# A hybrid decoder block on one Trainium2 core: transposes tied to emitted weight pieces, moves on GpSimd's queue, a gate and a z block in one product, and a shorter last root

## The chip, the cores and the metric

The kernel runs on one core of one Trainium2 chip, in one launch. The metric is the device time of one execution in microseconds (us); the time before is 1645.88 us, the median of three runs (1645.79 to 1647.56). Engines are called as in the profile: PE (TensorE, matrix products), DVE (VectorE), ACT (ScalarE), POOL (GpSimd) and SP (SyncE, which here only starts transfers). An engine, and a queue of transfers that it starts, takes its instructions in order.

## The reference

One layer over 256 tokens (two halves of 128, called t = 0 and 1), width D = 2048, all in float32. The three branches are sliding-window attention with sinks, a multi-scale pooling mixer and a Mamba-2 SSD mixer; the parts around the change are these:

```python
h = rmsnorm(x, ln1_w)
q, k, v, u, z, xbc, dt_raw, gate_logits = split(h @ w_in)
ssm = ssd_mixer(z, xbc, ...)
# in ssd_mixer: g = (y * silu(z)) in 4 groups of 512 columns,
#               g * rsqrt(mean(g*g) + EPS) * norm_w
gates = sigmoid(gate_logits)            # 3 x 2048
merged = gates[0] * (att @ w_attn_br) + gates[1] * (pool @ w_pool_br) \
       + gates[2] * (ssm @ w_ssm_br)
x = x + merged @ w_out
gu = rmsnorm(x, ln2_w) @ w_gate_up
x = x + (silu(gu[:, :F]) * gu[:, F:]) @ w_down
return rmsnorm(x, final_w)
```

## The kernel before

**Products.** Every float32 product is made of three passes in a rounded float32 form: each operand is cut into a high and a low part, and PE does high x high, high x low and low x high (`three`, L225 to L227). Weights arrive in pieces of two 128-row slices by 512 columns. For each piece ACT casts the high part `whi` and DVE subtracts it to get `wlo` (`split`, L139 to L147). `weights` (L149) has three buffers for the arriving `raw` and five each for `whi` and `wlo`. One piece is 2 slices x 2 token halves x 3 passes = 12 matmuls of 512 columns. A block is 512 output columns over K = 2048, that is 8 pieces or 96 matmuls.

**Double blocks.** `two_blocks` (L315) makes two blocks of 512 columns at once. For two of the eight pairs of slices it uses seven products in place of eight, so 21 matmuls where plain pieces have 24. Its banks are: q1 and q7 from the pool `tr`, q5 and q6 from `sm`, q2, q4, q3 and q8 from the four banks of `acc`. The operand's combinations (`block_forms`) are made once per operand as side work. The weights' combinations come through `sraw`, which has one buffer, and `vu` (`block_weights`, L288 on): `whi` and `wlo` of the first half of `sraw`, a DVE sum `vu`, its split, two more sums and two more splits.

**Transposes of activations.** A result has tokens on the partitions, and the next product needs its columns there. `turn` (L487 to L514) does this for a block of 512 columns: sixteen transfers of 32 KB put 32x128 pieces into `mid` (`move`), then DVE does two stream transposes into `tt` (L502) and four splits with a scale follow (`parts`; on ACT these are the rows `ssm_hi<-tt`). Turned are the SSD result `ys` (tile `y`, through `ssm`), the merged sum `m4`, the residual `x2` (tile `x`) and the FFN's product `ff`.

**Side work.** `later` appends work to a list, `pause` appends an empty entry with a cost, and `side(share)` is called once for each weight piece: it takes the first entry if there is credit. A turn is `move`, then `pause(5)` (moves on SP) or `pause(12)` (moves on POOL), then `parts`; whatever stands behind a pause in the list waits too. `finish_tasks` empties the list. A scheduler then places each engine's instructions by its own estimates of when things are ready.

**Order around the change.** After the pooling mixer's three blocks with gates come `branch(1, 3, ...)` with `gate(1, 3)`, then four z blocks g = 0 to 3. For each, ACT makes `sz` = silu(z) from the block's two banks (L1019), DVE multiplies it into `ys[g]`, ACT sums the squares (`junk`, L1022), a root `rsg` follows as side work and DVE scales `ys[g]` (L1027), and `turn(ys[g])` is queued with its moves on SP, in the same queue as the weights. Then `two_gates(2, 0)` makes two gates, and `two_branches(0, ...)` multiplies the turned `ssm` by `w_ssm_br`. `two_gates(2, 2)`, `two_branches(2, ...)` and the turns of `m4` (moves on POOL), `w_out` with the turns of `x2` (moves on SP), then the FFN in three parts: in each, `gate_up` double blocks, turns of `ff` (moves on SP), and `w_down`. The last step is the final norm, whose root (`rsqrt`, L458 to L466) on 128x1 tiles is a chain of small steps on DVE and ACT: v = ss/D + part on DVE, a square root on ACT, a reciprocal, and one Newton step with v.

Of the kernel before, what the change touches and what calls it, by code (L numbers as in the profile page):

```python
# [71 lines left out]
def hybrid_block(ctx: ExitStack, tc: tile.TileContext, ins, out):  # L72
# [31 lines left out]
    def tr():  # L104
        return ps_tr.tile([P, NB], F32, tag="tr", name="tr")
# [10 lines left out]

    tasks = deque()
    spare = [0.0]

    def later(fn, cost=0.0):  # L120
        tasks.append((fn, cost))

    def pause(cost):
        tasks.append((lambda: None, cost))

    def side(share):
        spare[0] = min(spare[0] + share, 4.0)
        if tasks and spare[0] > 0:
            fn, cost = tasks.popleft()
            spare[0] -= cost  # L130
            fn()
# [47 lines left out]
    class Pairs:  # L179
# [3 lines left out]
        def __init__(self, n, name):  # L183
            self.t = [k4([2, 2, SEQ], F32R, name) for _ in range(n // 2)]
# [69 lines left out]
    def block_forms(a, pairs):  # L254

        out = {}

        def forms_of(p):
            y = k2([2, T, P], F32, "fy")
            for k in range(2):  # L260
                dve.tensor_tensor(
                    y[:, k].rearrange("p t s -> p (t s)"),
                    a.hi(2 * p + k).bitcast(F32), a.lo(2 * p + k).bitcast(F32), ALU.add,
                )
            f = k2([4, P], F32, "ff4")
            dve.tensor_tensor(f[:, 1], y[:, 0, 1], y[:, 1, 1], ALU.subtract)
            dve.tensor_tensor(f[:, 2], f[:, 1], y[:, 0, 0], ALU.subtract)
            dve.tensor_tensor(f[:, 0], f[:, 2], y[:, 1, 0], ALU.add)
            dve.tensor_tensor(f[:, 3], y[:, 0, 0], y[:, 0, 1], ALU.subtract)
            t = late.tile([P, 2, 4, P], F32R, tag="forms", name="forms", bufs=4)  # L270
            split(f, t[:, 0], t[:, 1])
            out[p] = t

        for p in pairs:
            later(lambda p=p: forms_of(p), 3.0)
        return out
# [210 lines left out]
    def turn(block, k0, dst, scale=None, queue=sp):  # L487
# [4 lines left out]
        dst.waiting.add(k0 // 4)  # L492

        def move():
            for i in range(4):
# [19 lines left out]
        pause(5.0 if queue is sp else 12.0)  # L515
        later(parts, 3.8)
# [402 lines left out]
    def two_gates(br, j):  # L919

        c0 = C_G + br * D + j * NB
        out = []
        for sums in two_blocks(h, h_forms, w_in, 0, (c0, c0 + NB), KD, False):
            sg = k4([T, NB], F32, "sg")
            for t, (q, more) in enumerate(sums):
                dve.tensor_tensor(more, q, more, ALU.add)
                act.activation(sg[:, t, :], more, AF.Sigmoid, scale=rstd1[:, t:t + 1])
            out.append(sg)
        return out
# [12 lines left out]
    def two_branches(j, sgs):  # L942

        for n, sums in enumerate(two_blocks(ssm, s_forms, ins["w_ssm_br"][0], 0, (j * NB, (j + 1) * NB), KD)):
# [66 lines left out]
    branch(1, 3, po, ins["w_pool_br"][0], gate(1, 3))  # L1011
# [4 lines left out]
    for g in range(GROUPS):  # L1016
        for t, a in enumerate(tokens_block(h, KD, plain_loads(w_in, 0, C_Z + g * NB, NB), NB)):
            sz = k2([NB], F32, "sz")
# [5 lines left out]
        def finish(g=g):  # L1024
# [5 lines left out]
        turn(ys[g], 4 * g, ssm, lambda k: norms[:, 0, k:k + 1])  # L1030

        if g == 0:
            s_forms = block_forms(ssm, (0, 1))

    sgs = two_gates(2, 0)
    finish_tasks()
# [19 lines left out]
    def residual(j, accs):  # L1056
# [4 lines left out]
        turn(x2[j], 4 * j, x2p, lambda k: norms[:, 1, k:k + 1])  # L1061
# [83 lines left out]
    dve.tensor_scalar(part, part, 1.0 / D, EPS, ALU.mult, ALU.add)  # L1145
    out_v = out[0].rearrange("(t p) c -> p t c", p=P)
    for t in range(T):
# [10 lines left out]
        rstd = rsqrt(ss, D, [1], "rs3", part[:, t:t + 1])  # L1158
# [37 lines left out]
```

## Time and profile before

| | us |
|---|---|
| runs (median; all) | 1645.88; 1645.79, 1645.88, 1647.56 |
| the profiled execution's own time | 1648.74 |
| its span in the trace | 1646.6 |
| PE busy in the span | 1626.4 (99%) |
| DVE busy | 1318.8 (80%) |
| ACT busy | 898.2 (55%) |
| POOL busy | 96.8 (6%) |
| mean granted clock of PE | 0.998 |

Every time of the trace is counted from the span's start in the profiled execution. Lines L142 and the like are lines of the kernel before. A number in brackets behind a row is the engine's idle time just before it and what ended it. The granted clock is a share of full speed.

### The profile page before, as it was taken

How to read it: one execution, taken by the hardware profiler on the slowest of the kernel's cores; microseconds unless marked ns; L12 is line 12 of the kernel's file. 1: busy time of each engine (PE TensorE's matmuls, PEld its weight loads, DVE VectorE, ACT ScalarE, POOL GpSimd, SP SyncE). 2: the span in 40 equal slices, each digit the busy share in tenths (PEclk: the TensorE clock that was granted, in tenths of full speed). 3: DMA queues.
4: the chain of work that ended last, by engine and by line, in shares of the span. 5: the costliest groups of instructions: out<-in, count | busy, mean ns of one | idle time of the engine just before them, and what ended most of it. 6: DMA issues, size and time to landing. Idle time of an engine off the chain costs nothing.

```text
span 1646.6 us, 20971 instructions
## 1 busy us (share of the span) xinstructions
PE 1626.4 (99%) x7689; PEld 1349.5 (82%) x7689; DVE 1318.8 (80%) x1738; ACT 898.2 (55%) x1190; POOL 96.8 (6%) x126
## 2 busy tenths in 40 slices
PE   8999999999999999999999999999999999999998
PEld 7888888888888888778888878888888888888887
DVE  5789898964786557688886799988879888888986
ACT  5467678644554457554545565554445555445553
POOL 1000001210220100002230000000000000000000
PEclk9999999999999999999999999999999999999999
DMA  8654566546566556566866666666666666666663
GB/s 250 204 159 146 166 196 205 179 158 200 161 224 212 197 185 212 155 233 203 265 221 191 202 211 226 206 215 215 204 205 193 219 214 217 205 203 199 216 212 103
DMA packets 214088, 328.83 MB, mean 200 GB/s; under 512 B 16253, under 2 KB 86145, under 8 KB 213985
## 3 DMA queue, kind: packets, MB, share of 16 engines
q1 hardware_dynamic: 209056, 317.77, 59.2%
q0 software_dynamic: 4176, 8.86, 1.9%
q8 instruction: 60, 0.98, 0.2%
q10 hardware_dynamic: 752, 0.86, 0.2%
q14 instruction: 44, 0.35, 0.1%
HBM read 313.25 MB, written 2.13 MB: 192 GB/s over the span
## 4 chain that ended last, share of the span: by engine, by line
PE 86%; SPq 4%; DMA 4%; DVE 3%; issue 1%; ACT 1%; DVEq 0%; ACTq 0%
PE acc L225 19%; PE acc L227 19%; PE acc L226 19%; PE acc L383 9%; PE acc L384 4%; SPq L497 4%; PE sm L226 2%; PE tr L227 2%; PE tr L226 2%; PE tr L225 2%; PE sm L225 2%; PE sm L227 2%; DVE wlo L143 1%; DMA raw<-in_w_gate_up_dram 1%; PE sm L868 1%
## 5 line engine op out<-in xcount | busy, mean ns | idle before, releaser
L143 DVE TENSOR_TENSOR wlo<-raw,whi 128x1024 fp32r<-128x1024 f32 (+2 forms) x500 | 600.2, 1215 | 155.8 <-ACT whi L142 154.7
L142 ACT CAST whi<-raw 128x1024 fp32r<-128x1024 f32 (+2 forms) x500 | 509.1, 1035 | 361.9 <-PE acc L227 244.3
L383 PE MATMUL acc<-h,whi 128*128 128x512 f32 x640 | 228.4, 400 | 0.0
L226 PE MATMUL acc<-wlo,x2p_hi 128*128 128x512 f32 x572 | 223.2, 390 | 1.2 <-DVE wlo L143 1.2
L225 PE MATMUL acc<-whi,x2p_hi 128*128 128x512 f32 x572 | 223.3, 390 | 0.0
L227 PE MATMUL acc<-whi,x2p_lo 128*128 128x512 f32 x572 | 223.0, 390 | 0.0
L226 PE MATMUL acc<-wlo,h 128*128 128x512 f32 (+1 forms) x508 | 195.5, 386 | 5.8 <-DVE wlo L143 5.7
L225 PE MATMUL acc<-whi,h 128*128 128x512 f32 (+1 forms) x508 | 196.9, 390 | 2.3 <-ACT whi L142 1.9
L227 PE MATMUL acc<-whi,h 128*128 128x512 f32 (+1 forms) x508 | 194.6, 386 | 0.0
L384 PE MATMUL acc<-h,wlo 128*128 128x256 f32 x640 | 180.3, 282 | 0.0
L142 ACT CAST whi<-sraw 128x1024 fp32r<-128x1024 f32 x84 | 88.1, 1049 | 121.8 <-PE acc L227 96.1
L383 PEld LDWEIGHTS acc<-h,whi 128*128 128x128 f32 x640 | 120.2, 188 | 30.1 <-issue 1.5
L143 DVE TENSOR_TENSOR wlo<-sraw,whi 128x1024 fp32r<-128x1024 f32 x84 | 102.6, 1221 | 45.4 <-ACT whi L142 45.2
L226 PEld LDWEIGHTS acc<-wlo,x2p_hi 128*128 128x128 f32 x572 | 107.4, 188 | 25.0 <-DVE wlo L143 2.3
L227 PEld LDWEIGHTS acc<-whi,x2p_lo 128*128 128x128 f32 x572 | 107.4, 188 | 23.0
L225 PEld LDWEIGHTS acc<-whi,x2p_hi 128*128 128x128 f32 x572 | 107.3, 188 | 23.0
L384 PEld LDWEIGHTS acc<-h,wlo 128*128 128x128 f32 x640 | 120.8, 189 | 1.8 <-issue 1.8
L226 PEld LDWEIGHTS acc<-wlo,h 128*128 128x128 f32 x508 | 95.8, 189 | 26.4 <-DVE wlo L143 7.2
L225 PEld LDWEIGHTS acc<-whi,h 128*128 128x128 f32 x508 | 95.6, 189 | 23.0 <-ACT whi L142 2.1
L227 PEld LDWEIGHTS acc<-whi,h 128*128 128x128 f32 x508 | 95.2, 188 | 19.4
L225 PE MATMUL acc<-whi,f_hi 128*128 128x512 f32 x244 | 95.3, 391 | 0.0
L227 PE MATMUL acc<-whi,f_lo 128*128 128x512 f32 x244 | 95.1, 390 | 0.0
(364 smaller groups left out, 2635.1 us busy)
## 6 DMA issues: line engine op xcount, KB each, us to landing
raw<-in_w_in_dram SPq DMA_DIRECT2D x80, 1024.0 KB, 5.3
raw<-in_w_gate_up_dram SPq DMA_DIRECT2D x132, 512.0 KB, 4.8
raw<-in_w_down_dram SPq DMA_DIRECT2D x62, 512.0 KB, 5.0
sraw<-in_w_gate_up_dram SPq DMA_DIRECT2D x44, 512.0 KB, 4.6
raw<-in_w_in_dram SPq DMA_DIRECT2D x43, 512.0 KB, 4.7
raw<-in_w_ssm_br_dram SPq DMA_DIRECT2D x24, 512.0 KB, 5.6
sraw<-in_w_down_dram SPq DMA_DIRECT2D x20, 512.0 KB, 5.0
raw<-in_w_attn_br_dram SPq DMA_DIRECT2D x8, 1024.0 KB, 5.1
```

Of the source, the lines that this page charges most:

```text
L142: a = act.copy(hi, src)
L143: b = dve.tensor_tensor(lo, src, hi.bitcast(F32), ALU.subtract)
L225: pe.matmul(o, lhsT=xh, rhs=yh, start=first, stop=False)
L226: pe.matmul(o, lhsT=xh, rhs=yl, start=False, stop=False)
L227: pe.matmul(o, lhsT=xl, rhs=yh, start=False, stop=last)
L383: pe.matmul(accs[c], lhsT=hi[:, j, cols], rhs=a.both(k), start=k == 0, stop=False)
L384: pe.matmul(accs[c][:, :SEQ], lhsT=lo[:, j, cols], rhs=a.hi(k), start=False, stop=k == KD - 1)
L497: queue.dma_start(mid[32 * j:32 * j + 32, i], block[32 * i:32 * i + 32, :, j * P:(j + 1) * P])
L868: pe.matmul(p[:, i * HD:(i + 1) * HD], lhsT=mt[:, i, :], rhs=xdt[:, i, :], start=True, stop=True)
```

## The change

There are four edits.

1. `later` takes a condition `ready`, and `side` takes the first entry that is ready, not the first. The pauses are gone: `parts` of a turn is ready when five (moves on SP) or seven (moves on POOL) weight pieces have been emitted since its `move`. `forms_of` is ready when its operand no longer waits for a turn; `Pairs` gets a set `waiting` for that.
2. The turns of `ys` and `x2` issue their sixteen moves on POOL's queue, where those of `m4` were before. Those of `ff` stay on SP.
3. The gate (1, 3) and z block 0 are made by one `two_blocks` call over `h`, and `branch(1, 3)` comes behind it, on two `tr` banks. The silu of z block 0 is written in place. `finish_tasks()` ahead of `two_branches(0)` is gone.
4. In the last root ACT takes the square root of `ss` with scale 1/D and `part` as its bias, DVE makes -v/2 beside it (`halves` prepares its constant), and the Newton step has two operations in place of three.

```diff
--- before.py
+++ after.py
@@ -114,21 +114,26 @@
 
 
 
+
     tasks = deque()
-    spare = [0.0]
-
-    def later(fn, cost=0.0):
-        tasks.append((fn, cost))
+    spare, pieces = [0.0], [0]
+
+    def later(fn, cost=0.0, ready=None):
+        tasks.append((fn, cost, ready))
 
     def pause(cost):
-        tasks.append((lambda: None, cost))
+        later(lambda: None, cost)
 
     def side(share):
+        pieces[0] += 1
         spare[0] = min(spare[0] + share, 4.0)
-        if tasks and spare[0] > 0:
-            fn, cost = tasks.popleft()
-            spare[0] -= cost
-            fn()
+        if spare[0] > 0:
+            for i, (fn, cost, ready) in enumerate(tasks):
+                if ready is None or ready():
+                    del tasks[i]
+                    spare[0] -= cost
+                    fn()
+                    return
 
     def finish_tasks():
         while tasks:
@@ -181,6 +186,7 @@
 
 
         def __init__(self, n, name):
+            self.waiting = set()
             self.t = [k4([2, 2, SEQ], F32R, name) for _ in range(n // 2)]
 
         def need(self, k):
@@ -272,7 +278,7 @@
             out[p] = t
 
         for p in pairs:
-            later(lambda p=p: forms_of(p), 3.0)
+            later(lambda p=p: forms_of(p), 3.0, lambda p=p: p // 2 not in a.waiting)
         return out
 
     def block_loads(w, k, cols, moved):
@@ -490,8 +496,10 @@
 
         mid = k4([4, T, P], F32, "mid")
         dst.waiting.add(k0 // 4)
+        moved = []
 
         def move():
+            moved.append(pieces[0])
             for i in range(4):
                 for j in range(4):
                     queue.dma_start(mid[32 * j:32 * j + 32, i], block[32 * i:32 * i + 32, :, j * P:(j + 1) * P])
@@ -512,8 +520,7 @@
             dst.waiting.discard(k0 // 4)
 
         later(move)
-        pause(5.0 if queue is sp else 12.0)
-        later(parts, 3.8)
+        later(parts, 3.8, lambda: moved and pieces[0] - moved[0] >= (5 if queue is sp else 7))
 
 
     h = Pairs(KD, "h")
@@ -919,14 +926,14 @@
     def two_gates(br, j):
 
         c0 = C_G + br * D + j * NB
-        out = []
-        for sums in two_blocks(h, h_forms, w_in, 0, (c0, c0 + NB), KD, False):
-            sg = k4([T, NB], F32, "sg")
-            for t, (q, more) in enumerate(sums):
-                dve.tensor_tensor(more, q, more, ALU.add)
-                act.activation(sg[:, t, :], more, AF.Sigmoid, scale=rstd1[:, t:t + 1])
-            out.append(sg)
-        return out
+        return [gate_of(sums) for sums in two_blocks(h, h_forms, w_in, 0, (c0, c0 + NB), KD, False)]
+
+    def gate_of(sums):
+        sg = k4([T, NB], F32, "sg")
+        for t, (q, more) in enumerate(sums):
+            dve.tensor_tensor(more, q, more, ALU.add)
+            act.activation(sg[:, t, :], more, AF.Sigmoid, scale=rstd1[:, t:t + 1])
+        return sg
 
     def branch(br, j, a_parts, w, sg, banks=None):
         if br == 0:
@@ -941,7 +948,7 @@
 
     def two_branches(j, sgs):
 
-        for n, sums in enumerate(two_blocks(ssm, s_forms, ins["w_ssm_br"][0], 0, (j * NB, (j + 1) * NB), KD)):
+        for n, sums in enumerate(two_blocks(ssm, s_forms[0], ins["w_ssm_br"][0], 0, (j * NB, (j + 1) * NB), KD)):
             for t, (q, more) in enumerate(sums):
                 dve.tensor_tensor(more, q, more, ALU.add)
                 dve.tensor_tensor(more, more, sgs[n][:, t, :], ALU.mult)
@@ -1008,32 +1015,42 @@
     sgs = two_gates(1, 1)
     branch(1, 1, po, ins["w_pool_br"][0], sgs[0], [tr(), tr()])
     branch(1, 2, po, ins["w_pool_br"][0], sgs[1], [sm(), sm()])
-    branch(1, 3, po, ins["w_pool_br"][0], gate(1, 3))
 
 
     ssg = tiny([T, GROUPS], "ssg", 1)
     ssm = Parts(KD, "ssm")
-    for g in range(GROUPS):
-        for t, a in enumerate(tokens_block(h, KD, plain_loads(w_in, 0, C_Z + g * NB, NB), NB)):
-            sz = k2([NB], F32, "sz")
+    s_forms = []
+
+    def gated(g, accs, in_place=False):
+
+        for t, a in enumerate(accs):
+            sz = a if in_place else k2([NB], F32, "sz")
             act.activation(sz, a, AF.Silu, scale=rstd1[:, t:t + 1])
             dve.tensor_tensor(ys[g][:, t, :], ys[g][:, t, :], sz, ALU.mult)
             junk = k2([NB], F32, "junk")
             act.activation(junk, ys[g][:, t, :], AF.Square, accum_out=ssg[:, t, g:g + 1])
 
-        def finish(g=g):
+        def finish():
             rstd = rsqrt(ssg[:, :, g], NB, [T], "rsg")
             for t in range(T):
                 dve.tensor_scalar(ys[g][:, t, :], ys[g][:, t, :], rstd[:, t:t + 1], None, ALU.mult)
 
         later(finish, 1.5)
-        turn(ys[g], 4 * g, ssm, lambda k: norms[:, 0, k:k + 1])
-
+        turn(ys[g], 4 * g, ssm, lambda k: norms[:, 0, k:k + 1], pool)
         if g == 0:
-            s_forms = block_forms(ssm, (0, 1))
+            s_forms.append(block_forms(ssm, (0, 1)))
+
+
+    both = two_blocks(h, h_forms, w_in, 0, (C_G + D + 3 * NB, C_Z), KD, False)
+    sg = gate_of(both[0])
+    for q, more in both[1]:
+        dve.tensor_tensor(more, q, more, ALU.add)
+    gated(0, [more for _, more in both[1]], True)
+    branch(1, 3, po, ins["w_pool_br"][0], sg, [tr(), tr()])
+    for g in range(1, GROUPS):
+        gated(g, tokens_block(h, KD, plain_loads(w_in, 0, C_Z + g * NB, NB), NB))
 
     sgs = two_gates(2, 0)
-    finish_tasks()
     two_branches(0, sgs)
     sgs = two_gates(2, 2)
     mp = Parts(KD, "mp")
@@ -1058,7 +1075,7 @@
             dve.tensor_tensor(x2[j][:, t, :], a, x2[j][:, t, :], ALU.add)
             junk = k2([NB], F32, "junk")
             act.activation(junk, x2[j][:, t, :], AF.Square, accum_out=ss2[:, t, j:j + 1])
-        turn(x2[j], 4 * j, x2p, lambda k: norms[:, 1, k:k + 1])
+        turn(x2[j], 4 * j, x2p, lambda k: norms[:, 1, k:k + 1], pool)
         if j == 0:
             forms.append(block_forms(x2p, (0, 1)))
 
@@ -1143,6 +1160,8 @@
     part = tiny([T], "part", 1)
     dve.tensor_reduce(part, ss3, AX.X, ALU.add)
     dve.tensor_scalar(part, part, 1.0 / D, EPS, ALU.mult, ALU.add)
+    halves = tiny([T], "halves", 1)
+    dve.tensor_scalar(halves, part, -0.5, None, ALU.mult)
     out_v = out[0].rearrange("(t p) c -> p t c", p=P)
     for t in range(T):
         tok = slice(t * P, (t + 1) * P)
@@ -1155,7 +1174,14 @@
         junk = k2([256], F32, "junk")
         ss = tiny([1], "ss_last")
         dve.scalar_tensor_tensor(junk, x_, 1.0, x_, ALU.mult, ALU.mult, accum_out=ss)
-        rstd = rsqrt(ss, D, [1], "rs3", part[:, t:t + 1])
+        rstd, more = tiny([1], "rs3_r"), part[:, t:t + 1]
+        act.activation(rstd, ss, AF.Sqrt, scale=1.0 / D, bias=more)
+
+        half, q = tiny([1], "rs3_v"), tiny([1], "rs3_q")
+        dve.tensor_scalar(half, ss, -0.5 / D, halves[:, t:t + 1], ALU.mult, ALU.add)
+        dve.reciprocal(rstd, rstd)
+        dve.scalar_tensor_tensor(q, rstd, half, rstd, ALU.mult, ALU.mult)
+        dve.scalar_tensor_tensor(rstd, q, 1.5, rstd, ALU.add, ALU.mult)
         dve.scalar_tensor_tensor(x_, x_, rstd, fw[7], ALU.mult, ALU.mult)
         sp.dma_start(out_v[:, t, 3 * NB + 256:], x_)
         act.mul(x2[3][:, t, :256], x2[3][:, t, :256], rstd)
```

How this moves instructions is shown at three places. A line number in the rows is that of the kernel they are taken from: L142, L145, L1019, L1022, L153, L293 and L497 before are L147, L150, L1028, L1031, L158, L299 and L505 now. `x16` says that sixteen like rows follow one another.

The first is ACT in the z stage, around the scaled split (`ssm_hi`) of turned group g = 1 and the silu (`sz`) of z block 2. Before:

```order
L142 CAST whi<-raw 128x1024 x3
L1019 ACT_TABLE_LOAD
L1019 ACTIVATE sz<-acc,rs_r 128x512
L142 CAST whi<-raw 128x1024
L1022 ACTIVATE junk,ssg<-y 128x512
L1019 ACTIVATE sz<-acc,rs_r 128x512
L142 CAST whi<-raw 128x1024
L145 ACTIVATE ssm_hi<-tt,norms 128x256 x4
L1022 ACTIVATE junk,ssg<-y 128x512
```

Now:

```order
L147 CAST whi<-raw 128x1024 x6
L150 ACTIVATE ssm_hi<-tt,norms 128x256 x2
L1028 ACT_TABLE_LOAD
L1028 ACTIVATE sz<-acc,rs_r 128x512
L150 ACTIVATE ssm_hi<-tt,norms 128x256 x2
L1031 ACTIVATE junk,ssg<-y 128x512
L1028 ACTIVATE sz<-acc,rs_r 128x512
L147 CAST whi<-raw 128x1024
L1031 ACTIVATE junk,ssg<-y 128x512
```

The first half of the split of group 1 now stands ahead of the table load and of both `sz` of z block 2, where before the whole split stood behind them.

The second is ACT one block later, around the split of group g = 2 and the first `sz` of z block 3, while the first combinations (`vu`, `sraw`) of `two_gates(2, 0)` are split. Before:

```order
L142 CAST whi<-vu 128x1024
L142 CAST whi<-sraw 128x1024
L142 CAST whi<-raw 128x1024
L1019 ACT_TABLE_LOAD
L1019 ACTIVATE sz<-acc,rs_r 128x512
L142 CAST whi<-raw 128x1024
L145 ACTIVATE ssm_hi<-tt,norms 128x256 x4
L1022 ACTIVATE junk,ssg<-y 128x512
```

Now:

```order
L147 CAST whi<-vu 128x1024
L147 CAST whi<-sraw 128x1024
L147 CAST whi<-raw 128x1024
L150 ACTIVATE ssm_hi<-tt,norms 128x256 x2
L1028 ACT_TABLE_LOAD
L1028 ACTIVATE sz<-acc,rs_r 128x512
L147 CAST whi<-raw 128x1024
```

Again two of the four splits went ahead of the first `sz`, which reads the bank `acc` of z block 3.

The third is SP's queue in the first FFN part, around the second of its sets of moves of `ff`, beside the loads of a `gate_up` double block. Before:

```order
L293 DMA sraw<-in_w_gate_up_dram 128x2x512 x2
L153 DMA raw<-in_w_gate_up_dram 128x2x512 x6
L293 DMA sraw<-in_w_gate_up_dram 128x2x512 x2
L153 DMA raw<-in_w_gate_up_dram 128x2x512
L497 DMA mid<-ff 32x2x128 x16
L153 DMA raw<-in_w_gate_up_dram 128x2x512 x5
```

Now:

```order
L299 DMA sraw<-in_w_gate_up_dram 128x2x512 x2
L158 DMA raw<-in_w_gate_up_dram 128x2x512 x6
L299 DMA sraw<-in_w_gate_up_dram 128x2x512
L505 DMA mid<-ff 32x2x128 x16
L299 DMA sraw<-in_w_gate_up_dram 128x2x512
L158 DMA raw<-in_w_gate_up_dram 128x2x512 x6
```

The sixteen moves went from between two plain loads to between the two halves of the load of `sraw`. The same change is made once in each of the other two FFN parts; their other sets of moves keep their places. In the z stage and in `w_out` the SP queue now has no moves at all.

## Rows read from the trace of the kernel before

**Rows 1.** Page, part 1: busy us, share of span, instructions of each engine.

```profile
PE 1626.4 (99%) x7689; PEld 1349.5 (82%) x7689; DVE 1318.8 (80%) x1738; ACT 898.2 (55%) x1190; POOL 96.8 (6%) x126
```

**Rows 2.** Waits of PE over the span: us in total, times, longest us.

```profile
PE acc L226 <- DVE wlo L143: 6.9, 4, 3.9
```

**Rows 3.** Windows: us, PE, PEld, DVE, ACT, POOL busy, PEclk, DMA share, GB/s.

```profile
702.00:712.00 10.00, 6.13 (x20) 4.60 (x19) 10.00 (x14) 5.06 (x8) 0.00 (x0) 0.83 0.77 275
...
712.00:880.00 168.00, 168.00 (x738) 138.27 (x738) 139.15 (x152) 86.14 (x92) 37.02 (x68) 1.00 0.69 223
```

**Rows 4.** Timeline, PE, 666 to 710: start us, us, instruction, [idle before <-releaser].

```profile
668.65 0.39 PE L225 MATMUL tr<-whi,h 128*128 128x512 f32 x1
...
672.83 0.39 PE L225 MATMUL acc<-shi,forms 128*128 128x512 f32 x1
...
681.24 0.50 PE L226 MATMUL acc<-wlo,h 128*128 128x512 f32 x1 [1.84 <-DVE wlo L143]
...
706.68 0.50 PE L226 MATMUL acc<-wlo,h 128*128 128x512 f32 x1 [3.87 <-DVE wlo L143]
```

**Rows 5.** Timeline, SP (q: its DMA queue), in the z stage and the FFN.

```profile
639.64 10.19 SPq L497 DMA_DIRECT2D mid<-y  x16
...
1025.77 10.35 SPq L497 DMA_DIRECT2D mid<-ff  x16
```

**Rows 6.** Timeline, DVE, in the z stage and before `w_out`.

```profile
638.69 0.88 DVE L1027 TENSOR_SCALAR y<-y,rsg_r 128x512 f32<-128x512 f32 x2
...
651.22 2.05 DVE L502 STREAM_TRANSPOSE tt<-mid 128x512 f32<-128x512 f32 x2 [1.55 <-DMA mid<-y]
...
658.91 0.88 DVE L1027 TENSOR_SCALAR y<-y,rsg_r 128x512 f32<-128x512 f32 x2
...
861.65 2.06 DVE L502 STREAM_TRANSPOSE tt<-mid 128x512 f32<-128x512 f32 x2 [4.41 <-DMA mid<-m]
...
873.36 2.06 DVE L502 STREAM_TRANSPOSE tt<-mid 128x512 f32<-128x512 f32 x2 [2.48 <-DMA mid<-m]
```

**Rows 7.** Timeline, ACT, 665 to 679 (z stage).

```profile
667.25 1.28 ACT L1019 ACT_TABLE_LOAD   x1
...
668.54 0.69 ACT L1019 ACTIVATE sz<-acc,rs_r 128x512 f32<-128x512 f32 x1
...
674.34 1.71 ACT L145 ACTIVATE ssm_hi<-tt,norms 128x256 fp32r<-128x256 f32 x4 [4.17 <-DVE tt L502]
...
675.96 0.62 ACT L1022 ACTIVATE junk<-y 128x512 f32<-128x512 f32 x1
```

**Rows 8.** Timeline, POOL, 840 to 880.

```profile
847.89 8.51 POOL L497 DMA_DIRECT2D mid<-m  x16 [41.94 <-ACT whi L142]
...
857.15 0.54 POOL L497 DMA_DIRECT2D mid<-m  x1 [0.74 <-issue]
```

**Rows 9.** DMA issues by tile: count, KB each, median us from issue to landing.

```profile
mid<-y SPq DMA_DIRECT2D x64, 32.0 KB, 1.9
...
mid<-m POOLq DMA_DIRECT2D x64, 32.0 KB, 4.7
...
sraw<-in_w_gate_up_dram SPq DMA_DIRECT2D x44, 512.0 KB, 4.6
```

**Rows 10.** Page, part 5: groups, busy us, mean ns of one, idle before, releaser.

```profile
L143 DVE TENSOR_TENSOR wlo<-raw,whi 128x1024 fp32r<-128x1024 f32 (+2 forms) x500 | 600.2, 1215 | 155.8 <-ACT whi L142 154.7
...
L142 ACT CAST whi<-raw 128x1024 fp32r<-128x1024 f32 (+2 forms) x500 | 509.1, 1035 | 361.9 <-PE acc L227 244.3
```

**Rows 11.** Timeline, first FFN part: PE, then DVE.

```profile
978.25 0.39 PE L225 MATMUL tr<-whi,x2p_hi 128*128 128x512 f32 x1
...
980.76 0.75 DVE L1106 SCALAR_TENSOR_TENSOR ff<-u,rs_r,ff 128x512 f32<-128x512 f32 x1
```

**Rows 12.** Timeline, DVE, 1638 to 1642 (last root).

```profile
1639.48 0.21 DVE L461 TENSOR_SCALAR rs_v<-ss_last,part 128x1 f32<-128x1 f32 x1
...
1640.36 0.16 DVE L465 TENSOR_TENSOR rs_q<-rs_q,rs_v 128x1 f32<-128x1 f32 x1
```

## Prediction

> **What bounds the kernel now.** I read the page's busy times first. PE is busy for 1626.4 of 1646.6 us [rows 1], so the kernel is bound by PE, and a change can win only what PE idles, what it computes too much, and the tail. The waits of PE come next: four waits for a `wlo`, 6.9 us together, the longest 3.9 [rows 2]. Then the windows: from 712 to 880 PE is busy for all 168.00 us, in 738 matmuls [rows 3], so one matmul of 512 columns costs 168.00/738 = 0.228 us, and a piece of twelve 2.73. From 702 to 712 PE is busy for 6.13 of 10 us at a granted clock of 0.83. The timeline of PE shows why: 3.87 us idle at 706.68, and another wait of 1.84 at 681.24 [rows 4].
>
> The SP and DVE rows show what ends late there. SP spends 10.19 us on sixteen moves of `y` [rows 5], DVE waits 1.55 for them ahead of its transposes [rows 6], and ACT waits 4.17 behind DVE at `ssm_hi` [rows 7]. Weights behind the moves arrive late and PE pays.
>
> **What goes away.** All four waits lie in the z, gate and `w_out` stages (the largest two at 681.24 and 706.68 [rows 4], the others, 1.2 together, near 945), which lose their moves from SP's queue: 6.9 us. The clock went with the longest: 10 us at 0.83 give 10 x 0.17 = 1.7; after the wait of 1.84 us no slow matmul is to be seen, so I count nothing there. Sum 8.6. The new double block has two seven-product pairs: 6 matmuls fewer, 6 x 0.228 = 1.4. The last root loses v (0.21) and the product with v (0.16) [rows 12] and their gaps of some 0.03 each: 0.4; its new half of -v runs while ACT takes the root. Together **-10.4**.
>
> **What comes: the z stage.** The moves are now issued on POOL, which has little else (96.8 us in all [rows 1]). The trace prices this with `m`: sixteen issues from 847.89 take 8.51 us [rows 8], and the transposes start at 861.65 after a DVE wait for the moves [rows 6]: 13.8 from the first issue, with 0.3 from data to issue 14.1. On SP the same took 639.57 (the end of the scaling at 638.69 + 0.88) to 651.22: 11.6 [rows 6]. The landing differs: 4.7 us on POOL's queue, 1.9 on SP's [rows 9]. I take 14.1, since that row is the same queue and transfer.
>
> [...]
>
> Such a latency is harmless where nothing waits behind the transposes. The order of the changed ACT says otherwise at two places, where `ssm_hi` now stands ahead of a silu.
>
> *Group 1.* PE starts `two_gates(2, 0)` at 668.65 [rows 4]; call that E3. A block is 96 x 0.228 = 21.8 us, so z block 2 ends at E2 = 646.85 and z block 1 at E1 = 625.05. y of group 1 is ready at 639.57, E1 + 14.5. From there: 14.1 to the transposes, 2.05 for them, half of `ssm_hi` 0.86, the table 1.28, silu 0.69, the other half 0.86, `junk` 0.62, silu 0.69 [rows 6, 7], then the cast 1.04 and `wlo` 1.22 of the piece behind it [rows 10]: 23.4, so E1 + 37.9. That piece is the fifth of z block 3; PE wants its second matmul after 21.8 + 4 x 2.73 + 0.2 = E1 + 32.9. Wait **5.0**.
>
> *Group 2.* y is ready at 658.91 + 0.88 = E2 + 12.9 [rows 6]. The first silu of z block 3 now stands behind half of `ssm_hi`: 14.1 + 2.05 + 0.86 + 1.28 + 0.69 = 19.0, E2 + 31.9. It frees the bank that q3 of the next double block takes. PE took q3 at 672.83 [rows 4], E2 + 26.0. Before, that silu ran at 668.54, ahead of the wait for the transposes [rows 7]. Wait **5.9**. The first wait moves both sides of the second, the gate later and the need later, by about as much.
>
> Both are longer than 3.87, so each brings the slow clock: 2 x 1.7. Sum **+14.3**.
>
> Bounds: with SP's 11.6 in place of 14.1 the waits are 2.5 and 3.4, with clock 0 to 3.4, so +5.9 to +9.3. The slowest set on POOL in the trace was issued from 857.15 [rows 8] and transposed at 873.36 [rows 6], 16.2 later, which makes them 7.1 and 8.0: +18.5.
>
> **What comes: the FFN.** In three places the second half of `sraw` now goes behind the sixteen moves of `ff`. In the pattern of the first part, PE starts the double block at T = 978.25 and `ff` is ready at 980.76 + 0.75, T + 3.3 [rows 11]. The moves take 10.35 [rows 5], the half lands 4.6 after its issue [rows 9]: T + 18.2. Then come six operations on DVE and ACT of 1.04 to 1.22 each [rows 10], 6.9 together: T + 25.1. PE has 21 matmuls of the first pair, six pieces and ten more matmuls of work ahead: 4.8 + 16.4 + 2.3 = T + 23.4. So 1.7 late by the median landing; some halves land a little earlier, and I take 1.2, three times: **+3.6**, with 0 and 6 as ends (6 needs each to be 2 us). The row at 681.24 argues that so short a wait keeps the clock.
>
> **At nothing.** The `x2` turns on POOL are covered by the pieces that DVE and ACT hold ready for PE (five `whi` and `wlo`, some 13 us); if that cover is short by 2 us at each of four, it costs 8. The `m` parts go from a pause of 12 to seven pieces, and may stall DVE by one or two us, which the same lead covers. `branch(1, 3)` on `tr` banks reads what is free by then. POOL's `m` products delay no move, since POOL is idle between them.
>
> **Sum.** -10.4 + 14.3 + 3.6 = **+7.5**. The profiled execution took 1648.74, with a span of 1646.6 and 2.1 around it, 2.9 above the median; nothing in the terms depends on that offset, so I set the change on the median: 1645.88 + 7.5 = **1653.4**.
>
> **The rivals.** *A, faster.* The transposes do not hold PE, since y is ready earlier than E1 + 14.5: before, its chain on DVE ran behind waits for SP's moves such as the 1.55 at 651.22 [rows 6], and these go. From data to transposes some 9 us (14.1 - 5.0) would do for group 1 and 8 for group 2, or y must come 5 to 6 us earlier. Then only the gains stay, with 0 to 3.6 in the FFN: 1635.5 to 1639.1. Against it: no set of moves was that quick in the trace, and the scaling stands behind pieces of split weights that fill DVE to 139 of 168 us [rows 3].
>
> *B, the same.* One of the two waits comes and the other is covered, say because the first delays the need of the second by more than its gate. -10.4 + 5.4 + 1.7 + 3.6 = +0.3, 1646.2; this holds if y comes earlier by 5 us in one group only.
>
> *C, slower still.* The FFN waits pass 2 us and drop the clock three times (3 x 1.7), and `x2` loses its cover at one or two turns: 1653.4 + 2.4 + 5.1 and some, 1661 and above. It decides where a wait in the FFN passes the 1.84 us that left the clock alone.
>
> *D, POOL is shut out.* If each of sixteen issues waited for one `wlo` of DVE (1.22), a set would take 16 x 1.22 = 19.5 us more, and twelve sets with half of it uncovered put the time past 1700. The row of POOL says no: 8.51/16 = 0.53 per issue [rows 8] while DVE was busy for 139.15 of 168 us [rows 3]. [...] 1 in 100, within slower.
>
> *E, the change does not do what it says.* The scheduler places `parts` by its own estimates, so the seven pieces may be fewer: in the order, DVE and ACT reach the transposes after some five pieces. That is inside my sum already.
>
> **How the numbers follow.** Forecast (both z waits) with what lies beside it 0.43, C and D 0.07, B 0.21, A 0.29. A measurement of this kernel tells 0.2% from no change, 3.3 us: 1642.6 to 1649.2. The forecast's own range is 1649.5 to 1660. Faster is A, 0.29, and 0.01 of B, 0.30; the same is the rest of B, 0.20; slower is the forecast with C and D, 0.50. The range leaves out the fast end of A and most of C and D, reaching to 1637.0 and to 1660.5.
>
> **What would show it.** In the profile of the changed kernel, PE's waits would name a `wlo` in z block 3 (some 5 us) and ACT's `sz` at the start of `two_gates(2, 0)` (some 6), with slow matmuls behind each; the four old waits should be gone, and PE should have 6 matmuls fewer. DVE at `tt` should wait for `mid<-y` by POOL's queue, with 13 to 16 us from first issue to the first transpose. In the FFN, three waits of PE of 1 to 2 us for a `wlo` of `sraw`. The forecast is wrong if y of groups 1 and 2 is ready over 5 us earlier after its block's end, if the transposes start within 9 us of it, or if PE waits elsewhere.

## The result, and the profile after

The changed kernel takes 1655.71 us (median of four runs, 1653.95 to 1657.06) against 1646.0 (1645.79 to 1647.56, four runs) measured beside it: ratio 1.0055, with the interval 1.0039 to 1.0071, or 9.7 us more. The forecast was 1653.4, 7.5 more. The profiled execution took 1657.06 us, with a span of 1655.2, 8.6 more than before.

The page's first part, busy us and instructions as in [rows 1]:

```profile
PE 1628.6 (98%) x7683; PEld 1349.3 (82%) x7683; DVE 1330.1 (80%) x1755; ACT 898.9 (54%) x1195; POOL 164.0 (10%) x254
```

PE has six matmuls fewer, as said, though it is busy for 2.2 us more. POOL is busy for 67.2 us more, which is the 128 issues that came to it. The time went into waits, and the waits of PE (us in total, times, longest), rows of which answer to [rows 2], say which:

```profile
PE acc L231 <- ACT sz L1028: 7.9, 1, 7.9
...
PE sm L232 <- DVE wlo L148: 3.2, 5, 0.8
...
PE acc L232 <- DVE wlo L148: 1.8, 3, 0.8
...
PE sm L231 <- ACT whi L147: 0.7, 2, 0.3
...
PE tr L233 <- DVE mp_lo L148: 0.5, 1, 0.5
...
PE tr L232 <- DVE wlo L148: 0.4, 1, 0.4
```

The four old waits, 6.9 us, are gone. In their place stands one wait of 7.9 us for a silu (`sz`), where there was none, and many of at most 0.8, the larger half of them on the `sm` banks, which take the seven-product pairs. PE's timeline, as in [rows 4]: the start of z block 1, the two waits in the z stage, the matmul after the longer one, and one in the FFN:

```profile
601.40 0.39 PE L231 MATMUL acc<-whi,h 128*128 128x512 f32 x1
...
657.73 0.50 PE L232 MATMUL acc<-wlo,h 128*128 128x512 f32 x1 [0.76 <-DVE wlo L148]
...
680.75 0.80 PE L231 MATMUL acc<-shi,forms 128*128 128x512 f32 x1 [7.86 <-ACT sz L1028]
...
681.35 0.63 PE L232 MATMUL acc<-slo,forms 128*128 128x512 f32 x1
...
1050.51 0.50 PE L232 MATMUL sm<-wlo,forms 128*128 128x512 f32 x1 [0.76 <-DVE wlo L148]
```

E1, the end of z block 1, is 601.40 + 21.8 = 623.2, and E2 by the same step is 645.0 (in the trace z block 3 starts at 645.31, since PE lost 0.3 at 623.64; the two offsets from E2 given below, 16.2 and 27.9, are both that much too long). The wait forecast at z block 3's fifth piece is at 657.73, only 0.76 long (forecast 5.0). The wait forecast for q3 of `two_gates(2, 0)` is at 680.75, 7.86 long (forecast 5.9). The window behind it (columns as in [rows 3]) shows the clock, granted at 0.69:

```profile
680.00:690.00 10.00, 9.25 (x29) 7.44 (x30) 9.16 (x16) 9.96 (x18) 0.00 (x0) 0.69 0.46 135
```

Eleven matmuls in a row stand 0.427 apart there, from 681.35 on, in place of 0.228: 11 x 0.2 = 2.2 us; after the 0.76 there is none. ACT's timeline around the two waits, as in [rows 7]:

```profile
650.50 0.91 ACT L150 ACTIVATE ssm_hi<-tt,norms 128x256 fp32r<-128x256 f32 x2 [6.66 <-DVE tt L510]
...
652.73 0.69 ACT L1028 ACTIVATE sz<-acc,rs_r 128x512 f32<-128x512 f32 x1
...
677.79 0.91 ACT L150 ACTIVATE ssm_hi<-tt,norms 128x256 fp32r<-128x256 f32 x2 [10.35 <-DVE tt L510]
...
680.01 0.69 ACT L1028 ACTIVATE sz<-acc,rs_r 128x512 f32<-128x512 f32 x1
```

ACT is idle for 6.66 and 10.35 us ahead of a split, with a silu behind it each time. DVE's timeline of the same stretch, as in [rows 6], has the scaling and the transposes of both groups:

```profile
634.23 0.88 DVE L1036 TENSOR_SCALAR y<-y,rsg_r 128x512 f32<-128x512 f32 x2
...
648.41 2.06 DVE L510 STREAM_TRANSPOSE tt<-mid 128x512 f32<-128x512 f32 x2 [5.99 <-DMA mid<-y]
...
660.31 0.88 DVE L1036 TENSOR_SCALAR y<-y,rsg_r 128x512 f32<-128x512 f32 x2
...
675.72 2.04 DVE L510 STREAM_TRANSPOSE tt<-mid 128x512 f32<-128x512 f32 x2 [7.96 <-DMA mid<-y]
```

POOL's timeline has the moves between them, as in [rows 8]:

```profile
635.69 6.40 POOL L505 DMA_DIRECT2D mid<-y  x12 [20.99 <-issue]
...
643.71 2.13 POOL L505 DMA_DIRECT2D mid<-y  x4 [1.62 <-DMA mid<-y]
...
661.78 5.85 POOL L505 DMA_DIRECT2D mid<-y  x11 [15.94 <-ACT whi L147]
```

From issue to landing a move of `y` now takes 4.4 us in the median, on SP's queue 1.9 [rows 9]:

```profile
mid<-y POOLq DMA_DIRECT2D x64, 32.0 KB, 4.4
```

This is the chain of the forecast, with other sizes. y of group 1 is ready at 634.23 + 0.88 = 635.1, E1 + 11.9 (forecast 14.5), and transposed 13.3 us later, at 648.41 (forecast 14.1). The two halves of `ssm_hi` stand around the silu of z block 2, so that ends at 653.42, and y of group 2 is ready only at 661.19, E2 + 16.2 (forecast 12.9). It is transposed 14.5 us later, at 675.72; the silu of z block 3 ends at 680.70, and PE goes on 0.05 later. In the FFN the loads of `sraw` stand around the sixteen moves, which take 10.80 us:

```profile
1027.78 0.37 SPq L299 DMA_DIRECT2D sraw<-in_w_gate_up_dram  x1
1028.46 10.80 SPq L505 DMA_DIRECT2D mid<-ff  x16
1039.30 0.59 SPq L299 DMA_DIRECT2D sraw<-in_w_gate_up_dram  x1
```

Six waits of 0.3 to 0.8 follow in the three FFN parts (two, three and one), 3.4 together. The last root's chain of four DVE steps:

```profile
1648.26 0.21 DVE L1181 TENSOR_SCALAR rs_v<-ss_last,halves 128x1 f32<-128x1 f32 x1
1648.58 0.16 DVE L1182 RECIPROCAL rs_r<-rs_r 128x1 f32<-128x1 f32 x1
1648.78 0.22 DVE L1183 SCALAR_TENSOR_TENSOR rs_q<-rs_r,rs_v 128x1 f32<-128x1 f32 x1
1649.03 0.16 DVE L1184 SCALAR_TENSOR_TENSOR rs_r<-rs_q,rs_r 128x1 f32<-128x1 f32 x1
```

From the end of the sum of squares to the scaled result it is 1648.14 to 1649.23, 1.09 us, where before it was 1639.36 to 1640.74, 1.38: 0.3 less.

### The profile page after: what moved, and what is told of

The parts are those of the page before. It is cut to its first block, busy times and chain, and to the rows that moved or that the text cites. A ratio compares the mean times of both kernels' runs of the same rounds, so it can differ in the third digit from the quotient of the medians.

```text
span 1655.2 us, 20998 instructions
## 1 busy us (share of the span) xinstructions
PE 1628.6 (98%) x7683; PEld 1349.3 (82%) x7683; DVE 1330.1 (80%) x1755; ACT 898.9 (54%) x1195; POOL 164.0 (10%) x254
## 4 chain that ended last, share of the span: by engine, by line
PE 43%; DVE 6%; DMA 3%; SPq 2%; issue 2%; POOL 1%; ACT 1%; DVEq 0%; ACTq 0%
PE acc L232 12%; PE acc L233 12%; PE acc L231 12%; DVE wlo L148 2%; SPq L505 2%; PE tr L233 1%; PE tr L232 1%; PE tr L231 1%; PE sm L232 1%; PE sm L233 1%; PE sm L231 1%; DMA mid<-x 1%; POOL mid L505 1%; DMA mid<-m 1%; DMA sraw<-in_w_gate_up_dram 1%
## 5 line engine op out<-in xcount | busy, mean ns | idle before, releaser
L148 DVE TENSOR_TENSOR wlo<-raw,whi 128x1024 fp32r<-128x1024 f32 (+2 forms) x496 | 592.1, 1211 | 118.7 <-ACT whi L147 116.6
L147 ACT CAST whi<-raw 128x1024 fp32r<-128x1024 f32 (+2 forms) x496 | 502.3, 1034 | 320.5 <-PE acc L233 223.0
L231 PE MATMUL acc<-whi,h 128*128 128x512 f32 (+1 forms) x496 | 192.2, 390 | 0.8 <-ACT h L150 0.3
L232 PE MATMUL acc<-wlo,h 128*128 128x512 f32 (+1 forms) x496 | 191.1, 386 | 0.9 <-DVE wlo L148 0.8
L233 PE MATMUL acc<-whi,h 128*128 128x512 f32 (+1 forms) x496 | 190.1, 386 | 0.1
L147 ACT CAST whi<-sraw 128x1024 fp32r<-128x1024 f32 x88 | 92.5, 1051 | 125.6 <-PE acc L233 90.8
L148 DVE TENSOR_TENSOR wlo<-sraw,whi 128x1024 fp32r<-128x1024 f32 x88 | 107.8, 1225 | 46.3 <-ACT whi L147 45.9
L231 PEld LDWEIGHTS acc<-whi,h 128*128 128x128 f32 x496 | 93.5, 189 | 21.3 <-ACT h L150 1.7
L233 PEld LDWEIGHTS acc<-whi,h 128*128 128x128 f32 x496 | 93.0, 189 | 19.0 <-DVE h L151 0.3
L510 DVE STREAM_TRANSPOSE tt<-mid 128x512 f32<-128x512 f32 x46 | 47.9, 1071 | 63.4 <-DMA mid<-y 24.4
L232 PE MATMUL acc<-wlo,f_hi 128*128 128x512 f32 x244 | 95.1, 390 | 0.0
```

The source lines that it names most:

```text
L147: a = act.copy(hi, src)
L148: b = dve.tensor_tensor(lo, src, hi.bitcast(F32), ALU.subtract)
L231: pe.matmul(o, lhsT=xh, rhs=yh, start=first, stop=False)
L232: pe.matmul(o, lhsT=xh, rhs=yl, start=False, stop=False)
L233: pe.matmul(o, lhsT=xl, rhs=yh, start=False, stop=last)
L510: dve.transpose(tt.rearrange("p k (t i s) -> p t i k s", t=T, i=4)[:, t], mid[:, :, t].rearrange("p i (c k) -> p i k c", k=4),)
```

## The experiments

Each ran beside the kernel before on the same chip: runs 1 to 4 on one, 5 to 8 on a second, 9 and 10 on a third. Ratios are to the kernel before on that chip (medians 1648.2, 1648.0 and 1647.9), and only ratios are compared between chips. Counts are the weight pieces after which a turn's `parts` are ready. In the diffs `wait=` gives `turn` another count.

**1. ys ready after nine pieces.**

```diff
-turn(ys[g], 4 * g, ssm, lambda k: norms[:, 0, k:k + 1], pool)
+turn(ys[g], 4 * g, ssm, lambda k: norms[:, 0, k:k + 1], pool, wait=9)
```

> The changed kernel with one number other: the parts of the four ys turns are ready after nine emitted pieces, not seven; the moves stay on GpSimd's queue. In the order ACT then makes both silu of z blocks 2 and 3 ahead of the splits of groups 1 and 2. My theory (PE's bank and weights wait for a silu that stands behind a slow transpose): the wait of 7.9 us at 680.75, the 0.8 at 657.73 and the slow clock behind them go, 9 to 12 us: 1644 to 1647. Rival (the queue's latency itself costs, wherever its readers stand): the wait turns up again at the splits or at the first matmul of ssm, and the time stays at 1652 to 1656.

Measured: 1642.34 us, ratio 0.9967 (0.9955 to 0.998). PE's waits on the `acc` banks, columns as above:

```profile
PE acc L231 <- ACT whi L147: 0.6, 1, 0.6
...
PE acc L232 <- DVE wlo L148: 0.6, 1, 0.6
```

The timeline of ACT around both splits:

```profile
645.61 0.69 ACT L1029 ACTIVATE sz<-acc,rs_r 128x512 f32<-128x512 f32 x1
...
656.83 1.71 ACT L150 ACTIVATE ssm_hi<-tt,norms 128x256 fp32r<-128x256 f32 x4 [1.60 <-DMA mid<-y]
...
667.41 0.69 ACT L1029 ACTIVATE sz<-acc,rs_r 128x512 f32<-128x512 f32 x1
...
682.51 1.71 ACT L150 ACTIVATE ssm_hi<-tt,norms 128x256 fp32r<-128x256 f32 x4 [0.63 <-DVE tt L510]
```

Both silu (645.61, 667.41) run ahead of the splits (656.83, 682.51), no wait for `sz` is left, and the moves are still on POOL. One number turned the loss into a gain: the theory held and the rival fell. By the ratios of runs 1 and 5 it gave 0.0083 of 1648, 13.7 us, more than the 9 to 12 that I had written. Two waits of the changed kernel in `w_out`, 0.38 at 882.56 and 0.47 at 932.31, are gone as well, which I had not expected of this edit.

**2. ff ready after four pieces.**

```diff
-turn(a_, 4 * i, f)
+turn(a_, 4 * i, f, wait=4)
```

> The changed kernel with the parts of the ff turns ready after four emitted pieces, not five. In the order SP then issues both halves of sraw ahead of the sixteen moves of ff, as before the change. My theory (the second half of sraw is late behind the moves): the six waits in the FFN of 0.3 to 0.8 us go with what PE loses as it restarts, 3.4 to 5 us: 1650.5 to 1652.5. Rival (these waits come from elsewhere, DVE being too full): at most 1 us, 1654.7 or more.

Measured: 1649.38 us, ratio 1.0012 (1.0003 to 1.002). SP's timeline beside the same block:

```profile
1027.68 10.19 SPq L505 DMA_DIRECT2D mid<-ff  x16
1037.92 2.85 SPq L158 DMA_DIRECT2D raw<-in_w_gate_up_dram  x5
```

PE's waits for the silu and on `sm`:

```profile
PE acc L231 <- ACT sz L1029: 7.2, 1, 7.2
...
PE sm L232 <- DVE wlo L148: 0.8, 1, 0.8
```

The moves now stand with five `raw` loads behind them and both halves of `sraw` ahead, and all six FFN waits are gone; the wait for `sz` is still there, 7.2. The one left on `sm` is at 723.89, in `two_branches`. The theory held; by the ratios of runs 2 and 5 it gave 0.0038 of 1648, 6.3 us, with intervals of 1.4 and 2.1 us to either side, a little over the 3.4 to 5 expected.

**3. Both counts.** The edits of 1 and 2.

> Both counts together, nine for ys and four for ff. If the two losses are independent, as my theory has it, the gains add: 1639 to 1643, faster than the kernel before. Rival (the order of one stage hangs on the other, or the gains of the change are smaller than I counted): 1644 or more.

Measured: 1637.28 us, ratio 0.9937 (0.9923 to 0.995), 10.4 us under the kernel before by that ratio. The three waits that PE has left behind 500 us:

```profile
PE tr L231 <- ACT mp_hi L147: 0.9, 1, 0.9
...
PE acc L232 <- DVE wlo L148: 0.5, 1, 0.5
...
PE tr L233 <- DVE mp_lo L148: 0.5, 1, 0.5
```

The gains add: 5.1 us of ff (1642.34 to 1637.28, same chip) on top of that of ys. So the two losses are separate, and they hid a change that wins. It won more than the 1639 to 1643 expected.

**4. The last root alone.** The kernel before with the root's part of the diff.

> The kernel before with only the shorter last root. Theory: two small DVE steps and their gaps leave the tail, 0.2 to 0.4 us: 1645.6 to 1645.8. Rival (the tail ends on something else, the last copies to memory): no change, 1646.0.

Measured: 1646.23 us, ratio 0.9992 (0.9983 to 1.0002), which does not tell the two expectations apart. In its trace the last matmul starts 8.1 us ahead of the span's end, before 8.4.

**5. The changed kernel again.** No edit.

> The changed kernel itself, as a control beside the other runs of this call. Both theories: 0.4 to 0.7% above the kernel before, as measured first (1.0055); about 10 us slower than before.

Measured: 1656.08 us, ratio 1.005 (1.0037 to 1.0062). The loss repeats.

**6. The queue undone.**

```diff
-turn(ys[g], 4 * g, ssm, lambda k: norms[:, 0, k:k + 1], pool)
+turn(ys[g], 4 * g, ssm, lambda k: norms[:, 0, k:k + 1])
-turn(x2[j], 4 * j, x2p, lambda k: norms[:, 1, k:k + 1], pool)
+turn(x2[j], 4 * j, x2p, lambda k: norms[:, 1, k:k + 1])
```

> The changed kernel with its second edit undone: ys and x2 moved on SP's queue, ready after five pieces. In the order the whole split of group 1 stands ahead of the silu of z block 2, and that of group 2 behind the first silu of z block 3. My theory: the 7.9 us and the slow clock behind them go (11 us), the waits for weights behind SP's moves come back (9 us with clock), the FFN's 5 us stay: 3 us under the changed kernel to 2 over it. Rival (the 7.9 us come of the condition of edit 1, not of the queue): the wait for sz stays, and with SP's moves added the time is 8 us or more over the changed kernel.

Measured: 1663.69 us, ratio 1.0093 (1.0079 to 1.0107), 7.6 over the changed kernel on the same chip: a miss for both. The wait for `sz` went, as the theory had it, but what came back is larger than it had said. SP's timeline in `w_out`:

```profile
889.46 21.83 SPq L505 DMA_DIRECT2D mid<-x  x32
...
911.39 1.96 SPq L158 DMA_DIRECT2D raw<-in_w_out_dram  x3
```

PE's timeline there:

```profile
918.33 0.80 PE L231 MATMUL acc<-whi,mp_hi 128*128 128x512 f32 x1 [6.25 <-ACT whi L147]
```

Two sets of `x2` moves follow each other with no load between, 21.83 us of SP, and PE waits 6.25 for a `whi`. Before, the pauses kept three loads between the two sets. The condition of edit 1, which lets later work pass a turn that waits, took that away, by the code; with the 64 moves of `x2` on POOL's queue, as in the changed kernel, SP's queue carries none of them. Run 7 below keeps the pauses and has the same queues. The two differ by the first edit, the root and one `finish_tasks()`, and by the ratios by 13 us: with these counts the new list, on SP's queue, loses.

**7. The double block alone.** The kernel before with the third edit, on its old pauses and queues; only `finish_tasks()` ahead of `two_branches(0)` stays.

> The kernel before with only its third edit: gate (1, 3) and z block 0 as one double block. Theory: six matmuls of 0.228 us fewer, 1.4 us under the kernel before, if nothing else moves; the waits behind SP's moves stay. Rival (the edit moves the order of the z stage, and SP's moves fall on other loads): a change of 3 us or more either way.

Measured: 1649.4 us, ratio 1.0012 (1.0003 to 1.0021): 2 us slower, between the two expectations. PE's waits behind SP's moves:

```profile
PE acc L226 <- DVE wlo L143: 8.4, 5, 2.7
```

They were four with 6.9 us [rows 2]. The six matmuls are gone, but the order moved and SP's moves fall on other loads, 1.5 us worse and in more places. Six matmuls fewer and 1.5 us of waits more make about nothing, so the 2 us are not explained by them. The matmuls saved do not show alone.

**8. Nine and four, with ys and x2 on SP.** Run 3 with the diff of run 6. The count of `ys` stays nine and that of `ff` four, but that of `x2` follows its queue, from seven to five.

> The run with nine and four (e3_both) with ys and x2 moved on SP's queue in place of GpSimd's. ACT's order in the z stage stays but for one cast, so this prices the queue alone. My theory: SP's sixteen moves hold the weight loads behind them for 10 us each time, and the waits of the kernel before come back, 5 to 9 us over e3_both. Rival (the queue does not matter once the silu stands ahead of the splits): within 2 us of e3_both.

Measured: 1654.79 us, ratio 1.0039 (1.0026 to 1.0051), by the ratios 16.8 over run 3. SP's timeline in `w_out`:

```profile
886.12 21.53 SPq L505 DMA_DIRECT2D mid<-x  x32
...
907.75 1.96 SPq L158 DMA_DIRECT2D raw<-in_w_out_dram  x3
```

Two waits in PE's timeline:

```profile
700.41 0.80 PE L232 MATMUL acc<-wlo,h 128*128 128x512 f32 x1 [3.04 <-DVE wlo L148]
...
914.87 0.79 PE L231 MATMUL acc<-whi,mp_hi 128*128 128x512 f32 x1 [5.42 <-ACT whi L147]
```

With the silu placed well the queue, together with the count of `x2`, is worth some 17 us, more than the 5 to 9 expected: the old waits come back in the z stage (3.04 at 700.41), and `w_out` gets the new one of run 6 (5.42, behind 21.53 us of moves). So POOL's queue was the right place for these two, and its latency (3.4 us in the median for a move of `y` in run 3), with run 3's counts, leaves no wait for `ys` behind a silu.

**9. ys ready after eight pieces.** As run 1, with `wait=8`.

> The changed kernel with ys ready after eight pieces. In the order the split of group 1 stands behind both silu of z block 2, as in the run with nine, but half the split of group 2 still stands ahead of the silu of z block 3, as in the changed kernel. In that kernel y of group 2 was ready 16.2 us after the end of z block 2, in the run with nine 7.8. Theory A (the hold of the silu of block 2 made y of group 2 late, and that made the second wait): y comes some 8 us earlier, the wait of PE for sz falls from 7.9 to 0 to 2 us, slow clock gone: 9 to 12 us under the changed kernel. Theory B (my prediction's sentence: the first wait moves both sides of the second alike): the wait for sz stays at 6 to 8 us, at most 2 us under the changed kernel.

Measured: 1645.97 us, ratio 0.9991 (0.9983 to 1.0), 9.7 under the changed kernel by the ratios of runs 5 and 9. DVE's timeline around group 2:

```profile
651.79 0.88 DVE L1037 TENSOR_SCALAR y<-y,rsg_r 128x512 f32<-128x512 f32 x2
...
665.12 2.06 DVE L510 STREAM_TRANSPOSE tt<-mid 128x512 f32<-128x512 f32 x2 [1.45 <-DMA mid<-y]
```

ACT's:

```profile
667.22 0.91 ACT L150 ACTIVATE ssm_hi<-tt,norms 128x256 fp32r<-128x256 f32 x2 [2.08 <-DVE tt L510]
...
669.44 0.69 ACT L1029 ACTIVATE sz<-acc,rs_r 128x512 f32<-128x512 f32 x1
```

Half the split of group 2 (667.22) still stands ahead of the silu (669.44), but PE has no wait for it: y of group 2 is ready at 652.67, in the changed kernel at 661.19, and these 8.5 us are more than the wait of 7.86. So theory A held. The wait of 7.9 us was made one block earlier, where the split of group 1 held the silu of z block 2, though that hold itself cost PE next to nothing. Between run 1 and this one some 4 us remain by the ratios. PE's waits behind 500 us make 6.5 us here and 4.8 in run 1 (one of 0.46 at 696.23 and one of 0.76 at 713.43 are new), which is less than half of that; the rest stays open.

**10. The last m moves shared.** Run 3, with the odd `i` of `move` on SP for the last two m blocks.

```diff
-                    queue.dma_start(mid[32 * j:32 * j + 32, i], ...)
+                    (sp if half and i % 2 else queue).dma_start(mid[32 * j:32 * j + 32, i], ...)
```

> The run with nine and four (e3_both), where the sixteen moves of each of the last two m blocks go half on GpSimd's queue and half on SP's. Theory: the transposes of m come some 4 us sooner, and the waits of PE for mp_hi and mp_lo (0.9 and 0.5 us) go: 0.5 to 2 us under e3_both. Rival (SP's half holds the weight loads of w_out behind it): no gain, or slower by 1 to 5 us.

Measured: 1635.5 us, ratio 0.9928 (0.9914 to 0.9941). The waits for `mp_hi` and `mp_lo` are gone. It is 1.8 under run 3, which ran on another chip; by the ratios 1.5, and the two intervals overlap, so the gain is likely and not shown. This is the fastest version tried, some 12 us under the kernel before.

## Why the prediction was right, point by point

The mechanism held in kind: a silu held behind a split that waits for POOL's slower moves (4.4 us from issue to landing, 1.9 on SP's queue before), and loads of `sraw` held behind the moves of `ff`. That the number came so close is in part luck. Against the forecast, group 1 was 5.9 us too much, group 2 was 2.5 too little, what had been set at nothing or had no term was 2.7, and PE's restarts some 3; with 0.2 less in the FFN, these leave the 2.2 us between 7.5 and 9.7. Had one of them been otherwise, the number would have been off by several us with the same account.

- **The gains, -10.4.** The four waits and the eight slow matmuls behind the longest (0.43 us apart) went, and six matmuls (7689 to 7683). The root gave 0.3 of 0.4. Run 3 bears out the size: it gains 10.4 us with 2.0 us of new waits still in it.
- **Group 1, 5.0 + 1.7.** This term was too large: 0.76 and no slow clock. Of the 4.2 us, 2.6 are y, ready sooner after its block (11.9 for 14.5; I had taken it from the kernel before, where the split of group 0 starts on ACT at 625.25, just behind E1, and now it starts at 617.04), and 0.8 the moves (13.3 for 14.1); the last 0.8 is PE, which wanted that matmul only at 657.73 - 0.76 = 656.97, E1 + 33.8 (forecast 32.9). From issue to landing the two queues are 2.5 us apart in the median, 4.4 on POOL's now and 1.9 on SP's before.
- **Group 2, 5.9 + 1.7.** Too small: 7.86, and 2.2 for eleven slow matmuls. The step that failed is the sentence that the first wait moves both sides of the second alike. It did not: the silu of z block 2 was held, so y of group 2 came 3.3 us later than taken, and PE, which hardly waited in the first place, wanted q3 at 672.9, E2 + 27.9, only 1.9 later than I had it. Run 9 shows it by taking the first hold away. The two errors cancel in part: the z terms were forecast at 14.3 and measured at 0.8 + 7.9 + 2.2 = 10.9.
- **The FFN, +3.6.** Measured 3.4 in six waits; run 2 shows the cause, the second half of `sraw` behind the moves. In the two later parts the waits come at the same places. No clock drop followed: from 1050 to 1060, 1307 to 1317 and 1563 to 1573 the granted clock is 1.00.
- **At nothing: the `m` and `x2` turns.** This was wrong by 1.6 us: `w_out` has four waits of 0.2 to 0.5 us. Two of them are for `mp_hi` and `mp_lo`, and run 10 shows that they come of the moves of `m`: the lead that was to cover a stall of one or two us did not cover all of it. The other two went in run 1, which left `m` and `x2` as they were, so their cause is open. `two_branches(0)`, for which I had no term, has two more of 0.5 and 0.6, cause open too: 2.7 together.
- **What the waits leave out.** After each wait PE restarts with a matmul gap over 0.228 (0.34, behind the longest 0.60); read start to start, the waits are longer by 0.2 to 0.3 us each, some 4 us in all after and 0.9 before, which no term of mine held. With them the terms, as measured, come to -10.4 + 10.9 + 3.4 + 2.7 + 3.1 = 9.7, where the medians are 9.7 apart. The two traces are 8.6 apart: there the double block starts 0.9 sooner than its place before (548.11 for 548.97), though nothing ahead of it was changed. That is chance: in run 5, the same kernel, it starts at 549.04.
- **The rivals.** A (faster) has the time of run 3, with ys two pieces later and ff one sooner; it was not this kernel, and y did come sooner in group 1, but by 2.6 us, not 5 to 6. B was nearest in its form, with one of the two waits, but that one was longer than its price. C had no sign: no FFN wait is over 0.8 us and no slow matmul follows one. D had no sign: the 64 issues each of y, m and x on POOL take 0.54 us in the median, and in POOL's longest stop between moves of y, from 642.09 to 643.71, DVE is idle from 642.42 on.

## What to carry to other kernels

When a slow step (a transfer, a transpose) moves to a queue of its own, look for what now stands behind its readers on other engines, in their order: the slower moves of `ys` cost nothing by themselves here (run 3, with nine pieces, has no wait of PE for `sz` or `ssm` left), and a silu placed behind their readers cost some 10 us (7.9 of wait and 2.2 of slow matmuls). A hold that costs the bound engine nothing may still cost it one block later, through what the held instruction makes (here 0.76 us, then 7.86 a block later). And a threshold that is counted in emitted pieces is a knob: one or two pieces decide here between 0.5% lost and 0.6% gained.

## What the hardware showed that I had not expected

POOL's issues stop inside a set. Of sixteen issues of 0.54 each, POOL did 12 from 635.69 and then waited 1.62 us for its own earlier moves, and 11 from 661.78, so these sets took 10.2 and 9.4 us where sixteen issues alone take 8.6. The same queue did sixteen in a row in 8.51 before [rows 8], and again in run 1 from 654.20. The traces tell why. The records of the moves carry eight semaphores, 102 to 109, in turn, and each issue waits for the landing of the one eight before it: the issue at 643.71 follows the landing, at 643.42, of the one from 637.83, and all eighteen waits of POOL for a move in this trace (17.2 us) end like this, 0.28 us behind such a landing. In the row of sixteen from 847.89, in the kernel before, the one eight before had always landed, for the last at 853.48, ahead of 855.87. So these stops are the program's own waits, and come where landing is slow (5.6 us there, where eight issues take 4.3); what slowed the landing in some sets is open.

The length of a wait alone does not tell whether the slow clock follows. Two waits of run 7, in PE's timeline:

```profile
674.39 0.53 PE L226 MATMUL acc<-wlo,h 128*128 128x512 f32 x1 [2.66 <-DVE wlo L143]
...
707.15 0.50 PE L226 MATMUL acc<-wlo,h 128*128 128x512 f32 x1 [2.65 <-DVE wlo L143]
```

Behind the first, matmuls stand 0.43 us apart until 678.14, and the window from 670 to 680 has a granted clock of 0.83; behind the second they stand 0.23 apart, and from 700 to 710 it is 1.00. The forecast took waits longer than 3.87 to bring the slow clock; that held for the one such wait that came, and one of 2.66 brought it too.
